# Retention and expert layer on one core: three chunks held for the products by token tiles, rows of the gathered tile spread anew

## The chip, the cores and the metric

The kernel runs on one core of one Trainium2 chip. The metric is the time of one execution on the device in microseconds (us); less is better. Three runs of the kernel before gave 1871.47, 1871.71 and 1877.47 us, a median of 1871.71 us.

## The reference

One layer of a token generator with 512 tokens of width 1024 and 256 context tokens. Two token mixers (retention and a gated linear recurrence) are merged and projected; the result `x1` goes through a normalisation and into an expert layer, and a last normalisation follows. Only the expert layer and the last normalisation matter here:

```python
q = (xb @ wq).reshape(PEER_BLOCK, PEER_HEADS, 2, PEER_DHALF)
s = jnp.einsum('thpd,hpkd->thpk', q, keys)
s1, i1 = lax.top_k(s[:, :, 0], K)
s2, i2 = lax.top_k(s[:, :, 1], K)
cand = (s1[..., :, None] + s2[..., None, :]).reshape(PEER_BLOCK, PEER_HEADS, K * K)
top, ci = lax.top_k(cand, K)
e = take(i1, ci // K) * PEER_NKEYS + take(i2, ci % K)
g = jax.nn.softmax(top, axis=-1)
act = jax.nn.gelu(jnp.einsum('thkd,td->thk', u_tab[e], xb))
return jnp.einsum('thk,thkd->td', g * act, v_tab[e])
...
x = x + g2x * peer_ffn(hx2, ...)
return rms_norm(x, final_g)
```

Every token picks 128 (8 heads, 16 each) of 16384 experts; `u_tab` and `v_tab` hold one row of 1024 float32 values for each expert. All arithmetic is float32.

## The kernel before, in words

The 512 tokens are four tiles of 128. **Three tiles** (384 tokens, `ndt` = 3) take the expert layer as dense products over all 16384 experts, in 128 chunks of 128 experts. **The fourth tile** gathers the rows that its tokens picked: 128 rows of `u` (one for each of the 128 picks, 128 tokens at a time), then 128 rows of `v`.

A dense float32 product is made of three products of split operands (`mm3`): `split` writes the high part on ScalarE (ACT) and the low part on VectorE (DVE), and TensorE (PE) multiplies high by high, high by low and low by high.

*The first table, S stages (`s_stage`).* Stage j loads 512 KB of `uT`, splits them (`wh`, `wl`; `w` has 2 buffers, `wh` and `wl` 4), makes 24 products into one of two PSUM buffers `pS`, and ACT writes their gelu into `gt`, a ring of `RING` buffers. Chunks below `SPILL` are stored from there to DRAM (`gd`) and come back later as `gr`; the others stay in the ring until their chunk is used. So stage j needs the ring buffer of stage j - RING, and the PSUM buffer of stage j - 2.

*The table stage (lines 846 to 906).* For each dense tile, in 8 slots of 16 tokens, DVE makes four one-hot tiles (`ohB`, `ohAl`, `ohAh`, `ohAl`), PE multiplies them (`pw`, 32 products of 128 columns in a slot), ACT copies the weights into `stg`, and SyncE's queue (SP) stores 1 MB of them in DRAM (`wd`). S stages are woven in as the tiles go. The order of the tiles is 0, 1, 3, 2: at the third place stand the lists of the gathered tile (`gather_prep`), and with the last dense tile the first `GFIRST` rows of `u` are gathered, by GpSimd's queue (POOL) into one of 4 buffers `row`, 512 KB each, and multiplied on DVE.

*The product stage (lines 952 on).* For each of 128 chunks: its weights `wt` or `wu` (a table of 8 chunks, 1.5 MB read from `wd`, which waits for every store into `wd`), its gelus, their product `af`, the split `ah`, `al`; 512 KB of `v`, split into `vwh`, `vwl`; 18 products of 512 columns into `po`, 6 for each tile. S stages still to be made and rows still to be gathered are woven in: `done < GFIRST + GSTEPS * (n_ + 1) // 128`, that is 1.97 rows a chunk. Chunks 126 and 127 are held: their products are made tile by tile, and behind a tile's last one follows its `finish`: times `g2r`, plus `x1`, square and sum, root, times the reciprocal and `fgr`, and out. The gathered tile's `finish` comes when its rows are through.

The order of the instructions on each engine is set when the program is built, by a scheduler that plays the program through with its own durations. On the chip each engine runs its list in that order.

Of the kernel before, what the change touches and what calls it, by code (L numbers as in the profile page):

```python
# [11 lines left out]
F32 = mybir.dt.float32  # L12
F32R = mybir.dt.float32r
# [3 lines left out]
AF = mybir.ActivationFunctionType  # L17
OP = mybir.AluOpType
# [3 lines left out]
D = 1024  # L22
KT = 8
# [15 lines left out]
    _n += _w  # L39
NCOLS = _n  # L40
DT = 384
SPILL, RING = 52, 14
GFIRST, GSTEPS, SSTEPS = 10, 252, 124
AHEAD = 2
NROW = 4
TORD = (0, 1, 3, 2)
# [6 lines left out]
def block_kernel(ctx: ExitStack, tc: tile.TileContext, A):  # L53
    nc = tc.nc
    V, S, PE, G, SY = nc.vector, nc.scalar, nc.tensor, nc.gpsimd, nc.sync

    def f(ap):
        return ap.bitcast(F32)

    def split(hi, lo, src):  # L60
        S.activation(hi, src, AF.Copy)  # L61
        V.tensor_tensor(lo, src, f(hi), op=OP.subtract)  # L62

    def mm3(out, wh, wl, xh, xl, start, stop):
        PE.matmul(out, wh, xh, start=start, stop=False)  # L65
        PE.matmul(out, wh, xl, start=False, stop=False)  # L66
        PE.matmul(out, wl, xh, start=False, stop=stop)  # L67
# [5 lines left out]
    wst = ctx.enter_context(tc.tile_pool(name="wst", bufs=2, reuse_waits="tile"))  # L73
    wsp = ctx.enter_context(tc.tile_pool(name="wsp", bufs=4, reuse_waits="tile"))
# [8 lines left out]
    def load_split(src, st, sp):  # L83
        n, m = src.shape[1:]
        w = st.tile([128, n, m], F32, name="w", tag="w")
        SY.dma_start(w, src)
        wh = sp.tile([128, n, m], F32R, name="wh", tag="wh")
        wl = sp.tile([128, n, m], F32R, name="wl", tag="wl")
        split(wh, wl, w)
        return wh, wl  # L90
# [52 lines left out]
    hl = hp.tile([128, KT, NX], F32R, name="hl", tag="hl")  # L143
# [393 lines left out]
    with ExitStack() as es:  # L537
# [25 lines left out]
        for c in range(KT):  # L563
            for g, (sh_, sl_) in ((1, (lruh, lrul)), (0, (reth, retl))):
                if (c, g) not in early:
                    gate_tanh(c, g, mg)
                t = gates[c, g]
# [24 lines left out]
        for q, (pool, th, tl) in enumerate(((lm, "lruh", "lrul"), (mg, "reth", "retl"))):  # L592
            wo.append([pool.tile([128, 4, KT, 128], F32R, name=f"wo{t}", tag=t, bufs=1) for t in (th, tl)])
            for c in range(4):
                w = wst.tile([128, KT, 128], F32, name="w", tag="w")
# [6 lines left out]
        for hf in range(2):  # L602
# [29 lines left out]
            for c in range(0, KT, 2):  # L632
                pt = ps_of("ptok", psW)
                for i in range(2):
                    for q in range(2):
                        o = 128 * (2 * q + i)
# [124 lines left out]
    def s_more(n=1):  # L761
        nonlocal s_next
        for _ in range(n):
            if s_next < 128:
                s_stage(s_next)
                s_next += 1
# [28 lines left out]
    def gather_rows():  # L795
        for j in range(128):
            row = gp.tile([128, D], F32, name="row", bufs=4)
            G.indirect_dma_start(out=row, out_offset=None, in_=A["u"],  # L798
                                 in_offset=bass.IndirectOffsetOnAxis(ap=ei[:, j:j + 1], axis=0))
            V.scalar_tensor_tensor(row, row, 1.0, h2t, op0=OP.mult, op1=OP.mult, accum_out=act[:, j:j + 1])  # L800
            yield
        S.activation(act, act, AF.Gelu_apprx_tanh)
        V.tensor_tensor(act, act, gg, op=OP.mult)
        for j in range(128):
            row = gp.tile([128, D], F32, name="row", bufs=4)
            G.indirect_dma_start(out=row, out_offset=None, in_=A["v"],  # L806
                                 in_offset=bass.IndirectOffsetOnAxis(ap=ei[:, j:j + 1], axis=0))
            if j == 0:
                V.tensor_scalar(acc, row, act[:, j:j + 1], None, op0=OP.mult)
            else:  # L810
                V.scalar_tensor_tensor(acc, row, act[:, j:j + 1], acc, op0=OP.mult, op1=OP.add)  # L811
            yield

    with ExitStack() as es:
# [5 lines left out]
        for h0 in range(0, H, HG):  # L820
# [3 lines left out]
            for hf in range(2):  # L824
# [4 lines left out]
                for i, pq in enumerate(pqs):  # L829
# [4 lines left out]
                    for tt in range(2):  # L834
                        t = 2 * hf + tt
# [16 lines left out]
        gen = None  # L852
        for t in TORD:
            if t == ndt:
                gather_prep(p1)
                gen = gather_rows()
# [15 lines left out]
            for tg in range(128 // WG):  # L872
                stg = p1.tile([128, 128, WG], F32, name="stg", bufs=2)
                for t0 in range(0, WG, 16):
                    o = tg * WG + t0
# [31 lines left out]
    ph = gpx.enter_context(tc.tile_pool(name="ph", bufs=1, reuse_waits="tile"))  # L907
# [4 lines left out]
    def finish(t, src, xt):  # L912
        xo = gp.tile([128, D], F32, name="xo", tag="row", bufs=4)
        ss = gp.tile([128, 2], F32, name="ss", bufs=4)
        hs = [slice(512 * n, 512 * n + 512) for n in range(2)]
        for n, o in enumerate(hs):
            V.tensor_tensor(xo[:, o], src[:, o], g2r[:, o], op=OP.mult)
            V.tensor_tensor(xo[:, o], xo[:, o], xt[:, o], op=OP.add)
            S.activation(xt[:, o], xo[:, o], AF.Square, accum_out=ss[:, n:n + 1])
        V.tensor_tensor(ss[:, 0:1], ss[:, 0:1], ss[:, 1:2], op=OP.add)  # L920
        S.activation(ss[:, 0:1], ss[:, 0:1], AF.Sqrt, scale=1.0 / D, bias=epsc)
        V.reciprocal(ss[:, 0:1], ss[:, 0:1])
        for o in hs:
            V.scalar_tensor_tensor(xo[:, o], xo[:, o], ss[:, 0:1], fgr[:, o], op0=OP.mult, op1=OP.mult)
            SY.dma_start(A["out"][0, 128 * t:128 * t + 128, o], xo[:, o])

    def load_x1(t):
        if t in (1, 2):
            xt = ph.tile([128, D], F32, name="xt", tag="vw", bufs=2)
        else:  # L930
            xt = gp.tile([128, D], F32, name="xt", tag="row", bufs=4)
        SY.dma_start(xt, x1d[:, t])
        return xt
# [5 lines left out]
    order, q = [], 0  # L939
# [6 lines left out]
    def table(j):  # L946
        gr = j // WI
        if gr not in wts:
            wt = ph.tile([128, NG_, WI, WG], F32, name="wt" if WI * gr + WI > SPILL else "wu", bufs=2)
            SY.dma_start(wt, wd[:, :, WI * gr:WI * gr + WI, :])  # L950
            wts[gr] = wt
        return wts[gr]
# [3 lines left out]
    for n_, j in enumerate(order):  # L956
        ring = j >= SPILL
        while s_next < min(128, s_first + (128 - s_first) * (n_ + 1) // SSTEPS) or (ring and s_next <= j):
            s_more()
        if ring:  # L960
            a = Gs.pop(j)
        else:
            a = ph.tile([128, DT], F32, name="gr", bufs=2)
            SY.dma_start(a, gd[:, j])
        wt = table(j)
        v = ph.tile([128, D], F32, name="vw", bufs=2)
        vd = SY.dma_start(v, A["v"][128 * j:128 * j + 128])

        with tc.issue_after(vd.ins):
            table(order[min(n_ + 3, 127)])  # L970
        vh, vl = (ph.tile([128, D], F32R, name=f"vw{m}", bufs=2) for m in "hl")
        ah, al = (ph.tile([128, DT], F32R, name=f"a{m}", bufs=2) for m in "hl")
        split(vh, vl, v)
        af = ph.tile([128, DT], F32, name="af")
        paced = V.tensor_tensor(af.rearrange("p (g t) -> p g t", t=WG), a.rearrange("p (g t) -> p g t", t=WG), wt[:, :, j % WI], op=OP.mult)
        split(ah, al, af)
        last.append((ah, al, vh, vl))
        if n_ == 125:

            g2r, fgr = (wst.tile([128, KT, 128], F32, name=nm, tag="w").rearrange("p n m -> p (n m)") for nm in ("g2r", "fgr"))  # L980
            SY.dma_start(g2r, g2d.to_broadcast([128, D]))
            SY.dma_start(fgr, A["fg"].to_broadcast([128, D]))
            with tc.issue_after(paced.ins):
                S.activation(gp.tile([128, 1], F32, name="ws"), epsc, AF.Sqrt)
        if n_ != 126:
            for t in range(ndt):
                for n in range(2):
                    for i, (ah, al, vh, vl) in enumerate(last):
                        mm3(outs[t][:, 512 * n:512 * n + 512], ah[:, 128 * t:128 * t + 128], al[:, 128 * t:128 * t + 128],
                            vh[:, 512 * n:512 * n + 512], vl[:, 512 * n:512 * n + 512], n_ == 0, n_ == 127 and i == 1)  # L990
                if n_ == 127:
                    finish(t, outs[t], load_x1(t))
            last = []
        with tc.issue_after(paced.ins):
            while gen and done < GFIRST + GSTEPS * (n_ + 1) // 128:
                done += 1
                if next(gen, 1):
                    gen = None
                    finish(ndt, acc, load_x1(ndt))
# [64 lines left out]
```

## Time and profile before

| | |
|---|---|
| median of the three runs | 1871.71 us |
| profiled execution, its own time | 1868.65 us |
| span of its instructions | 1866.9 us |
| PE busy | 1812.8 us (97%) |
| DVE busy | 1511.8 us (81%) |
| ACT busy | 822.2 us (44%) |
| moved by DMA | 431.27 MB, 231 GB/s on the mean |

The profile is that of one execution. "Busy" counts the time in which an instruction of the engine ran; products on PE overlap, so the step from one start to the next is shorter than an instruction's length: a product of 384 columns starts every 0.17 us and lasts 0.34 us. "Idle before" a row, in square brackets, is time in which its engine did nothing, with what ended it. L61 is line 61 of the kernel. SPq rows are DMAs issued by SP.

### The profile page before, as it was taken

Reading aid. Unit: us, or ns where it says so; the run is one execution under the profiler, and the core shown is the slowest. Engines: PE = TensorE matmul, PEld = TensorE weight load, DVE = VectorE, ACT = ScalarE, POOL = GpSimd, SP = SyncE. Lnnn points to the kernel's source line nnn. Section 1 sums busy time; section 2 is a strip of 40 time slices with the busy share of each in tenths; the row PEclk is TensorE's granted clock in tenths of the full one; section 3 lists DMA queues with packets and bytes.
Section 4 is the critical chain, followed back from the end, with each engine's and each line's share of the span. In section 5 each row is a group of like instructions: output and inputs, shape, how many; then the busy total and the mean of one; then the engine's idle time right before and its main releaser. Section 6 shows DMA issues by size and latency. Waiting matters only on the chain.

```text
span 1866.9 us, 26880 instructions
## 1 busy us (share of the span) xinstructions
PE 1812.8 (97%) x9953; PEld 1598.3 (86%) x9953; DVE 1511.8 (81%) x2793; ACT 822.2 (44%) x1203; POOL 377.7 (20%) x327
## 2 busy tenths in 40 slices
PE   7899999999999999999999989999999999999997
PEld 3788888887878989999999978888888888888886
DVE  8988777788853679999988678877787878788788
ACT  4666575765222444445545433333333333333323
POOL 0000000000000000000031244444454444344440
PEclk9999999999999999999999999999999999999999
DMA  7122121215953433657778989999999899998985
GB/s 312 52 68 69 57 69 57 69 57 175 327 157 102 153 107 105 189 188 246 253 283 281 320 323 348 337 330 320 345 339 344 316 340 339 355 329 320 347 308 206
DMA packets 173320, 431.27 MB, mean 231 GB/s; under 512 B 14850, under 2 KB 84610, under 8 KB 168708
## 3 DMA queue, kind: packets, MB, share of 16 engines
q1 hardware_dynamic: 136324, 295.31, 47.0%
q0 software_dynamic: 36864, 134.23, 19.7%
q8 instruction: 78, 1.28, 0.3%
q14 instruction: 54, 0.44, 0.1%
HBM read 388.86 MB, written 40.64 MB: 230 GB/s over the span
## 4 chain that ended last, share of the span: by engine, by line
PE 75%; DVE 11%; DMA 9%; ACT 2%; issue 2%; SPq 0%; DVEq 0%; POOL 0%; ACTq 0%; POOLq 0%
PE po L65 9%; PE po L66 9%; PE po L67 9%; PE pS L65 8%; PE pS L66 8%; PE pS L67 8%; DMA vw<-in_v_dram 5%; DMA modb<-in_mod_t_dram 2%; DVE wl L62 2%; PE pw L893 1%; PE pw L894 1%; PE pu L66 1%; PE pu L67 1%; PE pu L65 1%; PE p L66 1%
## 5 line engine op out<-in xcount | busy, mean ns | idle before, releaser
L61 ACT ACTIVATE wh<-w 128x1024 fp32r<-128x1024 f32 (+1 forms) x216 | 224.9, 1043 | 340.8 <-PE pS L66 76.9
L65 PE MATMUL pS<-h2h,wh 128*128 128x384 f32 x1024 | 346.5, 338 | 2.4 <-ACT gt L753 2.2
L67 PE MATMUL pS<-h2h,wl 128*128 128x384 f32 x1024 | 345.5, 337 | 0.7 <-DVE wl L62 0.7
L66 PE MATMUL pS<-h2l,wh 128*128 128x384 f32 x1024 | 345.5, 337 | 0.0
L62 DVE TENSOR_TENSOR wl<-w,wh 128x1024 fp32r<-128x1024 f32 (+1 forms) x216 | 258.9, 1200 | 84.3 <-ACT wh L61 81.9
L798 POOL DMA_INDIRECT row<-in_u_dram,ei x128 | 190.3, 1487 | 564.3 <-DVE row L800 288.3
L66 PE MATMUL po<-vwl,ah 128*128 128x512 f32 x768 | 300.2, 391 | 0.0
L67 PE MATMUL po<-vwh,al 128*128 128x512 f32 x768 | 299.8, 391 | 0.0
L65 PE MATMUL po<-vwh,ah 128*128 128x512 f32 x768 | 267.0, 395 | 10.1 <-ACT vwh L61 10.1
L61 ACT ACTIVATE ah<-af 128x384 fp32r<-128x384 f32 x128 | 67.1, 524 | 382.1 <-PE po L66 261.1
L806 POOL DMA_INDIRECT row<-in_v_dram,ei x128 | 177.6, 1387 | 224.4 <-DVE acc L811 193.1
L65 PEld LDWEIGHTS pS<-h2h,wh 128*128 128x128 f32 x1024 | 192.6, 188 | 9.6 <-ACT gt L753 3.3
L62 DVE TENSOR_TENSOR vwl<-vw,vwh 128x1024 fp32r<-128x1024 f32 x128 | 156.3, 1221 | 53.3 <-ACT vwh L61 53.1
L67 PEld LDWEIGHTS pS<-h2h,wl 128*128 128x128 f32 x1024 | 192.5, 188 | 6.2 <-DVE wl L62 1.0
L66 PEld LDWEIGHTS pS<-h2l,wh 128*128 128x128 f32 x1024 | 192.6, 188 | 5.4
L65 PEld LDWEIGHTS po<-vwh,ah 128*128 128x128 f32 x768 | 143.0, 188 | 37.0 <-ACT vwh L61 11.7
L61 ACT ACTIVATE vwh<-vw 128x1024 fp32r<-128x1024 f32 x128 | 134.6, 1051 | 84.7 <-DMA vw<-in_v_dram 79.3
L66 PEld LDWEIGHTS po<-vwl,ah 128*128 128x128 f32 x768 | 144.3, 188 | 27.6 <-DVE vwl L62 0.4
L67 PEld LDWEIGHTS po<-vwh,al 128*128 128x128 f32 x768 | 144.4, 188 | 27.3
L811 DVE SCALAR_TENSOR_TENSOR acc<-row,act,acc 128x1024 f32<-128x1024 f32 x127 | 162.5, 1280 | 4.4 <-DMA row<-in_v_dram,ei 4.2
L800 DVE SCALAR_TENSOR_TENSOR row<-row,h2t 128x1024 f32<-128x1024 f32 x128 | 153.4, 1219 | 1.7 <-DMA row<-in_u_dram,ei 1.5
L62 DVE TENSOR_TENSOR al<-af,ah 128x384 fp32r<-128x384 f32 x128 | 71.1, 556 | 79.2 <-ACT ah L61 78.9
(368 smaller groups left out, 3489.5 us busy)
## 6 DMA issues: line engine op xcount, KB each, us to landing
w<-in_uT_dram SPq DMA_DIRECT2D x128, 512.0 KB, 4.8
vw<-in_v_dram SPq DMA_DIRECT2D x128, 512.0 KB, 6.6
w<-in_w_in_dram SPq DMA_DIRECT2D x48, 512.0 KB, 3.6
wd<-stg SPq DMA_DIRECT2D x24, 1024.0 KB, 6.0
modb<-in_mod_t_dram SPq DMA_DIRECT2D x32, 512.0 KB, 5.2
wt<-wd SPq DMA_DIRECT2D x10, 1536.0 KB, 15.9
gd<-gt SPq DMA_DIRECT2D x52, 192.0 KB, 3.3
gr<-gd SPq DMA_DIRECT2D x52, 192.0 KB, 6.7
```

The costliest lines, as they stand in the source:

```text
L61: S.activation(hi, src, AF.Copy)
L62: V.tensor_tensor(lo, src, f(hi), op=OP.subtract)
L65: PE.matmul(out, wh, xh, start=start, stop=False)
L66: PE.matmul(out, wh, xl, start=False, stop=False)
L67: PE.matmul(out, wl, xh, start=False, stop=stop)
L798: G.indirect_dma_start(out=row, out_offset=None, in_=A["u"], in_offset=bass.IndirectOffsetOnAxis(ap=ei[:, j:j + 1], axis=0))
L800: V.scalar_tensor_tensor(row, row, 1.0, h2t, op0=OP.mult, op1=OP.mult, accum_out=act[:, j:j + 1])
L806: G.indirect_dma_start(out=row, out_offset=None, in_=A["v"], in_offset=bass.IndirectOffsetOnAxis(ap=ei[:, j:j + 1], axis=0))
L811: V.scalar_tensor_tensor(acc, row, act[:, j:j + 1], acc, op0=OP.mult, op1=OP.add)
L893: PE.matmul(pw[:, i], B[:, xg, :, xi], Ah[:, xg, :, xi], start=True, stop=False)
L894: PE.matmul(pw[:, i], B[:, xg, :, xi], Al[:, xg, :, xi], start=False, stop=True)
```

## The change

- `SPILL` 52 to 53 and `RING` 14 to 13: one chunk more goes through DRAM, one buffer less in the ring.
- `GFIRST` 10 to 26: 26 rows of `u` with the last dense tile. Then none for chunks 0 to 3, two a chunk to chunk 103, 36 over the 22 chunks after it (1.64 each), the last at chunk 125. `SSTEPS` 124 to 118: S stages are spread over fewer chunks.
- `HELD` = 3: chunks 125 to 127 are held for products by tiles. Their `v` comes through the buffers `w`, `wh`, `wl` that the S stages have left; `ah` and `al` get 3 buffers. `g2r` and `fgr` move into the buffers `vwh` and `vwl`.
- In `finish` the product with `fgr` comes ahead of the root, as a product of two tensors; the reciprocal of the root comes last, half of the columns on ACT (`Copy` with a scale), half on DVE.

```diff
-SPILL, RING = 52, 14
-GFIRST, GSTEPS, SSTEPS = 10, 252, 124
+SPILL, RING = 53, 13
+GFIRST, GSTEPS, SSTEPS = 26, 236, 118
+HELD = 3
...
+        for o in hs:
+            V.tensor_tensor(xo[:, o], xo[:, o], fgr[:, o], op=OP.mult)
...
+        S.activation(xo[:, hs[0]], xo[:, hs[0]], AF.Copy, scale=ss[:, 0:1])
+        V.tensor_scalar(xo[:, hs[1]], xo[:, hs[1]], ss[:, 0:1], None, op0=OP.mult)
         for o in hs:
-            V.scalar_tensor_tensor(xo[:, o], xo[:, o], ss[:, 0:1], fgr[:, o], op0=OP.mult, op1=OP.mult)
...
+        if n_ < 128 - HELD:
+            v = ph.tile([128, D], F32, name="vw", bufs=2)
...
+            vh, vl = (t.rearrange("p n m -> p (n m)") for t in
+                      load_split(A["v"][128 * j:128 * j + 128].rearrange("p (n m) -> p n m", m=128), wst, wsp))
...
-        if n_ == 125:
-            g2r, fgr = (wst.tile([128, KT, 128], F32, name=nm, tag="w")...
+        if n_ == 126:
+            g2r, fgr = (ph.tile([128, D], F32, name=nm, tag=tag, bufs=2) for nm, tag in (("g2r", "vwh"), ("fgr", "vwl")))
...
-        if n_ != 126:
+        if n_ < 128 - HELD or n_ == 127:
...
+        rows = min(2 * max(0, n_ - 3), 200 + max(0, n_ - 103) * (GSTEPS - 200) // 22)
         with tc.issue_after(paced.ins):
-            while gen and done < GFIRST + GSTEPS * (n_ + 1) // 128:
+            while gen and done < min(GFIRST + rows, 256 + n_ // 126):
```

The scheduler's order moves with it. Lines of the changed kernel stand one to nine further down (L62 and L63 for L61 and L62, L754 for L753, L801 for L800, L984 for L975).

**ACT, from the last slots of the table stage to the first split of the product stage.** `stg` are the weights of a slot (four copies), `gt` the gelu of an S stage, `wh` the split of the next `uT`, `ah` the first split of chunk 0. Before:

```order
L895 ACTIVATE stg<-pw 128x128x4 x3
L61 ACTIVATE wh<-w 128x1024
L895 ACTIVATE stg<-pw 128x128x4
L61 ACTIVATE wh<-w 128x1024
L753 ACTIVATE gt<-pS 128x384
L61 ACTIVATE wh<-w 128x1024
L753 ACTIVATE gt<-pS 128x384
L61 ACTIVATE wh<-w 128x1024
L753 ACTIVATE gt<-pS 128x384
L61 ACTIVATE ah<-af 128x384
L61 ACTIVATE vwh<-vw 128x1024
L753 ACTIVATE gt<-pS 128x384
```

After:

```order
L754 ACTIVATE gt<-pS 128x384 x2
L62 ACTIVATE wh<-w 128x1024 x2
L896 ACTIVATE stg<-pw 128x128x4 x8
L62 ACTIVATE wh<-w 128x1024 x3
L62 ACTIVATE ah<-af 128x384
L754 ACTIVATE gt<-pS 128x384
L62 ACTIVATE vwh<-vw 128x1024
```

Three gelus stood between the last `stg` and the first `ah`; now none does. On PE it is the same: before, 116 products of S stages 63 to 67 stand between the last product `pw` of the table stage and the first `po`; now stage 67 is through ahead of the last `pw`, and behind it stand 21 products of stage 68, which waits for the PSUM buffer of stage 66, that is for the gelu that ACT now has behind `ah`.

**DVE, over the same place.** `row,act` is one gathered row's product, `wl` a split of `uT`, `af` the first instruction of chunk 0. Before:

```order
L884 TENSOR_TENSOR ohB<-iota,e2T 128x2048
L885 TENSOR_TENSOR ohAl<-iota,e1T 128x2048
L800 SCALAR_TENSOR_TENSOR row,act<-row,h2t 128x1024 x2
L62 TENSOR_TENSOR wl<-w,wh 128x1024
L886 TENSOR_TENSOR ohAh<-ohAl,ghT 128x2048
L887 TENSOR_TENSOR ohAl<-ohAl,glT 128x2048
L62 TENSOR_TENSOR wl<-w,wh 128x1024 x5
L975 TENSOR_TENSOR af<-gt,wt 128x384
L800 SCALAR_TENSOR_TENSOR row,act<-row,h2t 128x1024
L62 TENSOR_TENSOR al<-af,ah 128x384
```

After:

```order
L885 TENSOR_TENSOR ohB<-iota,e2T 128x2048
L886 TENSOR_TENSOR ohAl<-iota,e1T 128x2048
L801 SCALAR_TENSOR_TENSOR row,act<-row,h2t 128x1024
L888 TENSOR_TENSOR ohAl<-ohAl,glT 128x2048
L801 SCALAR_TENSOR_TENSOR row,act<-row,h2t 128x1024 x2
L887 TENSOR_TENSOR ohAh<-ohAl,ghT 128x2048
L801 SCALAR_TENSOR_TENSOR row,act<-row,h2t 128x1024
L63 TENSOR_TENSOR wl<-w,wh 128x1024 x2
L888 TENSOR_TENSOR ohAl<-ohAl,glT 128x2048
L63 TENSOR_TENSOR wl<-w,wh 128x1024 x3
L984 TENSOR_TENSOR af<-gt,wt 128x384
L63 TENSOR_TENSOR al<-af,ah 128x384
```

Rows stand between the one-hot tiles of every slot now, and two of the five splits `wl` moved ahead of the last one-hot tile.

**DVE at the end.** Before, from the gathered tile's last step to the first tile's root:

```order
L924 SCALAR_TENSOR_TENSOR xo<-xo,ss,fgr 128x512 x2
L62 TENSOR_TENSOR al<-af,ah 128x384
L62 TENSOR_TENSOR vwl<-vw,vwh 128x1024
L917 TENSOR_TENSOR xo<-po_10702,g2r 128x512 x2
L918 TENSOR_TENSOR xo<-xo,xt 128x512 x2
L917 TENSOR_TENSOR xo<-po_10703,g2r 128x512 x2
L918 TENSOR_TENSOR xo<-xo,xt 128x512
```

After:

```order
L63 TENSOR_TENSOR al<-af,ah 128x384
L918 TENSOR_TENSOR xo<-acc,g2r 128x512 x2
L919 TENSOR_TENSOR xo<-xo,xt 128x512 x2
L922 TENSOR_TENSOR xo<-xo,fgr 128x512 x2
L923 TENSOR_TENSOR ss<-ss 128x1
L925 RECIPROCAL ss<-ss 128x1
L927 TENSOR_SCALAR xo<-xo,ss 128x512
L918 TENSOR_TENSOR xo<-po_10751,g2r 128x512 x2
L919 TENSOR_TENSOR xo<-xo,xt 128x512 x2
```

The gathered tile (`acc`) is finished behind the last chunk's splits and straight ahead of the first dense tile; before, it was finished among the last chunks. On PE, 16 products follow the first dense tile's last one before, 20 now; the third tile's are the last in both.

## Rows read from the trace of the kernel before

**Rows 1.** The page, head and part 1: span, PE's busy time.
```profile
span 1866.9 us, 26880 instructions
PE 1812.8 (97%) x9953; PEld 1598.3 (86%) x9953; DVE 1511.8 (81%) x2793; ACT 822.2 (44%) x1203; POOL 377.7 (20%) x327
```

**Rows 2.** Stretches: length, busy PE, PEld, DVE, ACT, POOL; PE clock, DMA share, GB/s.
```profile
940.00:1062.00 122.00, 122.00 (x960) 118.23 (x959) 93.38 (x111) 58.09 (x99) 21.94 (x15) 1.00 0.83 292
1062.00:1855.00 793.00, 782.92 (x3749) 685.02 (x3747) 643.83 (x818) 278.38 (x386) 337.72 (x242) 1.00 0.94 329
1855.10:1866.90 11.80, 0.04 (x1) 0.00 (x0) 8.29 (x19) 3.37 (x11) 0.00 (x0) 0.63 0.35 133
...
1480.00:1600.00 120.00, 117.81 (x563) 102.47 (x562) 98.35 (x106) 39.42 (x55) 53.45 (x39) 1.00 0.98 341
```

**Rows 3.** One stretch, instructions on `pS` alone: length, busy PE, PEld, DVE, ACT.
```profile
1042.30:1062.05 19.75, 19.75 (x114) 19.75 (x115) 0.00 (x0) 1.41 (x3) 1.00 0.93 304
```

**Rows 4.** Timeline between table stage and product stage: start, length, engine, line, what.
```profile
1042.26 0.22 PE L894 MATMUL pw<-ohAl,ohB 128*128 128x128 f16 x1
...
1044.95 0.58 ACT L895 ACTIVATE stg<-pw 128x512 f32<-128x512 f32 x1
...
1045.55 0.33 SPq L898 DMA_DIRECT2D wd<-stg  x1
...
1050.61 0.62 SPq L950 DMA_DIRECT2D wt<-wd  x1
...
1059.98 0.56 DVE L975 TENSOR_TENSOR af<-gt,wt 128x384 f32<-128x384 f32 x1 [3.30 <-DMA wt<-wd]
...
1060.57 0.53 ACT L61 ACTIVATE ah<-af 128x384 fp32r<-128x384 f32 x1 [4.77 <-DVE af L975]
...
1062.48 0.68 PE L65 MATMUL po<-vwh,ah 128*128 128x512 f32 x2
```

**Rows 5.** DMA issues: engine, count, KB each, median us to landing.
```profile
row<-in_u_dram,ei POOLq DMA_INDIRECT x128, 8.0
...
g2r<-g2d SPq DMA_DIRECT2D x1, 512.0 KB, 12.8
fgr<-in_fg_dram SPq DMA_DIRECT2D x1, 512.0 KB, 5.2
```

**Rows 6.** The tile `wt`: its ten loads, issue to landing.
```profile
DMA to landing us min/median/max: 9.3/15.9/20.1
```

**Rows 7.** Waits of PE from 1060 us on: us in total, times, longest.
```profile
PE po L65 <- ACT vwh L61: 10.1, 5, 5.9
```

**Rows 8.** Timeline ahead of the longest of these waits.
```profile
1065.44 0.61 SPq L950 DMA_DIRECT2D wt<-wd  x1
...
1067.34 8.36 SPq L967 DMA_DIRECT2D vw<-in_v_dram  x1
...
1086.17 1.06 ACT L61 ACTIVATE vwh<-vw 128x1024 fp32r<-128x1024 f32 x1 [9.44 <-DMA vw<-in_v_dram]
```

**Rows 9.** Two stretches behind that wait, columns as in Rows 2.
```profile
1087.20:1090.40 3.20, 3.12 (x9) 2.70 (x10) 2.64 (x3) 1.49 (x3) 0.00 (x0) 0.55 0.30 72
1090.40:1093.00 2.60, 2.60 (x13) 2.17 (x12) 2.56 (x5) 1.07 (x1) 0.31 (x1) 1.00 0.84 279
```

**Rows 10.** Groups by line: busy us, mean ns; `L573` with min/median/max ns.
```profile
L800 DVE SCALAR_TENSOR_TENSOR row<-row,h2t 128x1024 f32<-128x1024 f32 x128 | 153.4, 1219 | 1.7 <-DMA row<-in_u_dram,ei 1.5
...
L573 DVE TENSOR_SCALAR t<-t x8: 419/420/423, 465.4 to 605.7; 128x512 f32<-128x512 f32 x8
```

**Rows 11.** Timeline of the end: DVE's first and last work on `po`, PE's last product.
```profile
1851.54 1.29 DVE L917 TENSOR_TENSOR xo<-po,g2r 128x512 f32<-128x512 f32 x2 [2.21 <-PE po L67]
1852.74 1.28 DVE L918 TENSOR_TENSOR xo<-xo,xt 128x512 f32<-128x512 f32 x2
...
1854.75 0.39 PE L67 MATMUL po<-vwh,al 128*128 128x512 f32 x1
...
1862.05 1.41 DVE L924 SCALAR_TENSOR_TENSOR xo<-xo,ss,fgr 128x512 f32<-128x512 f32 x2
```

More of the change, by code (lines that the diff above doesn't have):

```diff
@@ L965, in block_kernel @@
         wt = table(j)
[L966 to L973, printed above, removed]
+        ah, al = (ph.tile([128, DT], F32R, name=f"a{m}", bufs=HELD) for m in "hl")
+        if n_ < 128 - HELD:
+            v = ph.tile([128, D], F32, name="vw", bufs=2)
+            vd = SY.dma_start(v, A["v"][128 * j:128 * j + 128])
+            with tc.issue_after(vd.ins):
+                table(order[min(n_ + 3, 127)])
+            vh, vl = (ph.tile([128, D], F32R, name=f"vw{m}", bufs=2) for m in "hl")
+            split(vh, vl, v)
+        else:
+            vh, vl = (t.rearrange("p n m -> p (n m)") for t in
+                      load_split(A["v"][128 * j:128 * j + 128].rearrange("p (n m) -> p n m", m=128), wst, wsp))
         af = ph.tile([128, DT], F32, name="af")
@@ L977, in block_kernel @@
         last.append((ah, al, vh, vl))
-        if n_ == 125:
-            g2r, fgr = (wst.tile([128, KT, 128], F32, name=nm, tag="w").rearrange("p n m -> p (n m)") for nm in ("g2r", "fgr"))
+        if n_ == 126:
+            g2r, fgr = (ph.tile([128, D], F32, name=nm, tag=tag, bufs=2) for nm, tag in (("g2r", "vwh"), ("fgr", "vwl")))
             SY.dma_start(g2r, g2d.to_broadcast([128, D]))
             SY.dma_start(fgr, A["fg"].to_broadcast([128, D]))
+        if n_ == 127 - HELD:
             with tc.issue_after(paced.ins):
                 S.activation(gp.tile([128, 1], F32, name="ws"), epsc, AF.Sqrt)
-        if n_ != 126:
+        if n_ < 128 - HELD or n_ == 127:
             for t in range(ndt):
@@ L989, in block_kernel @@
                         mm3(outs[t][:, 512 * n:512 * n + 512], ah[:, 128 * t:128 * t + 128], al[:, 128 * t:128 * t + 128],
-                            vh[:, 512 * n:512 * n + 512], vl[:, 512 * n:512 * n + 512], n_ == 0, n_ == 127 and i == 1)
+                            vh[:, 512 * n:512 * n + 512], vl[:, 512 * n:512 * n + 512], n_ == 0, n_ == 127 and i == HELD - 1)
                 if n_ == 127:
```

## The prediction

> **What bounds the kernel now.** I read the page's head first: PE is busy 97% of 1866.9 us [rows 1], so the question is where PE waits. The stretches [rows 2] show it. In the last part of the table stage, 940 to 1062, PE never stops (122 of 122 us), DVE is busy 93.4 us, and the DMA engines move 292 GB/s at a share of 0.83. In the product stage, 1062 to 1855, PE lacks 10.1 of 793 us, at 329 GB/s and a DMA share of 0.94. PE's waits name the cause of all 10.1 us: five times a `po` product stood for the split of a `v` chunk, once for 5.9 us [rows 7]; ACT had stood 9.4 us for that chunk's DMA, which SP had issued behind a table load [rows 8]. Behind that stop the granted clock was 0.55 for 3.2 us, most of it at the lower level of 1.2 GHz: 9 products started, which take 9 x 0.20 us at the pace of the 13 behind them, so another 1.4 us [rows 9]. After PE's last product, at 1854.75 + 0.39 = 1855.14, 11.8 us follow for the last normalisation [rows 2, 11]. What a change can win is thus about 11.5 us of stops and a part of 11.8 us. What it can lose is any cover that lies over a wait today, and one big cover does.
>
> **The cover.** The product stage needs a table that is read from DRAM behind the last store of the table stage. The timeline [rows 4] gives that chain: last `pw` product 1042.26; its weights copied by 1045.53; store issued 1045.55; landed, and the table's load issued, 1050.61; landed, and `af` of chunk 0, 1059.98; `ah` 1060.57; first `po` 1062.48. That is 20 us, and PE doesn't feel them: 114 recorded S products (116 by the order) fill 19.75 us of it without a gap [rows 3].
>
> **Rows and S stages in the table stage.** 16 more rows of `u` lie there. DVE takes 1.22 us for one [rows 10]: 19.5 us on top of 93.4 of 122, so DVE still fits, with 9 us over. But the one-hot tiles come later, and the order of PE answers with more S products ahead of the last `pw`: 68.0 stages instead of 63.1, 4.9 stages x 24 products x 0.173 us (19.75 / 114 [rows 3]) = 20.4 us. PE does the same work ahead of the first `po`; the last `pw` just moves to its end, to about 1062.7.
>
> **The boundary: the term that decides.** Behind the last `pw` PE's list now has stage 68, and that stage waits for a PSUM buffer that is free only when a gelu of stage 66 has run, whose `gt` buffer is free only when `af` of chunk 0 has run. ACT has that gelu behind `ah`. So PE stands from the last `pw` to that gelu's end; behind the waiting product all of PE's list is queued. The wait: the last copy 1.2 us after the last `pw` (four copies stand together now; before, the last stood behind a split that waited for its DMA, and took 3.3), store to landing 5.06, table load to `af` 9.37, `af` to `ah` 0.59, `ah` and gelu together 1.0: **17.2 us**. Bounds: the 9.37 is the shortest of ten such loads, whose median is 15.9 [rows 6], so 16 from below and 23.8 from above. I take the short one: it is the load of this same place, and SP holds the loads listed behind it back until the store has landed, now as before. After such a stop the clock restarts low, as in [rows 9]: +1.4. Together +18.6.
>
> The Trainium skill (DMA: Bandwidth & Descriptors, Anatomy of one DMA) prices a transfer at 2.0 us plus bytes over 436 GB/s, 5.6 us for this table of 1.5 MB, and the term would be 3.8 us less; this case's trace disagrees, with no load of the ten under 9.3 us [rows 6].
>
> **DMA in the table stage.** 16 rows x 0.524 MB = 8.4 MB more on 35.6 MB (122 us x 292) make 44.0 MB. No stretch of 120 us here moves more than 341 GB/s [rows 2]; at that rate they need 129 us, 7 us more than PE's work. A part can run on behind the last `pw`, while PE stands anyway, so I take +3, with 0 and +8 as ends (the upper end for rows that land late and hold up DVE's one-hot tiles, whose list they stand in; a row's landing takes 8.0 us [rows 5]).
>
> The Trainium skill (DMA: Bandwidth & Descriptors, Specifications) gives a core some 358 GB/s of HBM; by that this term would be 1 us. No 120 us here come near it; whether they could, no run shows.
>
> **The product stage.** 8.4 MB leave it, and chunks 0 to 3 have no rows. The stop at 1087, 5.9 + 1.4 us, came behind a second table, among gathered rows. The rows are gone; but the second table is now issued ahead of the second `v` chunk, and PE's order has only 4 S products between chunks 0 and 1. From the first table's landing, 2.1 MB (table and `v`) at 329 GB/s are 6.4 us at least, and 11 at the pace of the first table; PE has 21 x 0.173 + 18 x 0.23 = 7.7 us of work till then. I take a stop of 3 us in place of 7.3: -4.3 (ends -7.3 and 0). The four other stops, 4.2 us [rows 7], were of the same kind; in the middle there are 2 rows a chunk instead of 1.97, and S stages come faster, so transfers per PE time are the same; the end, with 1.64 rows, is easier. I take -1.4 (ends -4.2 and +4). The spilled chunk adds 0.4 MB, 1.2 us of DMA beside PE: nothing.
>
> **The end.** The first tile's last product stands 20 products ahead of PE's end instead of 16, not the 36 that "by tiles" suggests; 4 x 0.23 = 0.9 us earlier. DVE, which sets the end, works without a break from 1851.54 to 1863.46 [rows 11]. A tile's work on it was four tensor products at 0.60 (two start in 1.20) and two of 0.70; now six at 0.60 and one scale of 0.42 [rows 10], +0.2 a tile. The last step after the root falls from 1.41 to 0.42 beside ACT's half. I take -0.5. The gathered tile's `finish` now stands on DVE ahead of the first dense tile's, and `g2r` for it can be loaded only when chunk 123's products are done, 72 products, 72 x 0.23 = 16.5 us, ahead of PE's end. With the 5.2 us of `fgr` [rows 5] it lands 11 us ahead, its DVE work (3.6 + 0.4, root and table load about 2) is through 5 us ahead, just in time. With the 12.8 of `g2r` it costs 7 us. Ends -1.5 and +7.
>
> **The sum.** +18.6 + 3 - 4.3 - 1.4 - 0.5 = +15.4. On the profiled execution, 1868.65, that is 1884; the median lies 3.1 us above it, so 1887. I put 1886, since the low ends of two terms are the nearer ones.
>
> **Rivals.** *Not slower: the boundary at its lowest, and every stop gone.* The product stage keeps its rows short, all 11.5 us of stops vanish, the boundary costs 16 without a slow restart, the table stage nothing, the end -1.5: +3, 1875. For it speaks that all five stops name a `v` transfer and 8.4 MB leave; against it that the middle is as dense as before. It decides for "no change" below +5.6 us. To be faster, the boundary would have to be under 8 us, less than table load and copies alone; only a wait that I misread would do it (that stage 68 doesn't wait for the gelu). 13% for no change, 9% for faster.
>
> *Transfers take over in the table stage.* Rows and `uT` share a full DMA: the stage ends 8 us later, and the table load takes the median 15.9: 8 + 25.2 - 4.3 - 1.4 - 0.5 = +27, 1899. For it: 361 GB/s would be needed, over what any 120 us here show. Against: the rows can wait, and PE's S products have 4 split buffers. 15%.
>
> *The end waits for `g2r`*: +7 on the forecast, 1893. For it the 12.8 us, against it that this load met rows and `v` transfers, which are over by then. 8%.
>
> **How the numbers follow.** Forecast with its own range of 1877 to 1895: 55%. About 0.3%, 5.6 us, is what a measurement of this kernel can tell from no change. Slower 0.55 + 0.15 + 0.08 = 0.78, same 0.13, faster 0.09. The range leaves out the faster case, the low edge of the one without change and the upper half of the second rival, just under 2 in 10: 1869 to 1900.
>
> **What would show it.** In the profile after: PE idle once for 14 to 20 us at about 1063 to 1083, ahead of a `pS` product, ended by ACT's `gt`, with the wait of `af` for `wt` behind it; no S product between the last `pw` and that gap. GB/s in the 120 us ahead of it up from 292 to about 340. The stop behind the first chunk shorter than 7 us. DVE's first work on `po` 4.5 us ahead of PE's end, the end 11 to 11.5 us after it. The prediction is wrong if PE goes from `pw` to `po` without that gap, or if the last `pw` comes well ahead of 1060.

## The result, and the profile after

The changed kernel takes **1905.5 us**, the median of four runs (1901.1 to 1909.8); the kernel before took 1872.5 beside it. The ratio is 1.0166, with a 95% interval of 1.0145 to 1.0188; it is not the quotient of the two medians (1.0176), and in the table of the experiments the two can differ by 0.2%. The forecast was 1886, with a range of 1869 to 1900: the sign was right, and the time lies above the range.

Head and part 1 of its page, to be held against [rows 1]; PE is busy 10 us longer for the same number of products:

```profile
span 1908.0 us, 26901 instructions
PE 1822.8 (96%) x9953; PEld 1603.8 (84%) x9953; DVE 1513.8 (79%) x2797; ACT 825.2 (43%) x1207; POOL 377.7 (20%) x327
```

Stretches, columns as in [rows 2]: the 120 us up to the last `pw`, and the part of them that ran at half clock; the gap behind it; the product stage from the gap on, and its stretch behind one stop; the end.

```profile
950.00:1070.00 120.00, 114.52 (x841) 109.31 (x840) 97.43 (x125) 47.73 (x81) 41.52 (x26) 0.96 0.84 297
1062.00:1068.60 6.60, 6.24 (x21) 6.08 (x21) 1.02 (x1) 0.57 (x2) 0.00 (x0) 0.50 0.92 322
1070.90:1088.80 17.90, 0.16 (x3) 0.00 (x1) 4.55 (x5) 4.99 (x9) 0.00 (x0) 0.63 0.88 269
...
1088.80:1894.50 805.70, 789.53 (x3744) 688.31 (x3744) 625.42 (x787) 276.69 (x384) 320.99 (x226) 0.99 0.89 312
1188.80:1194.60 5.80, 5.80 (x15) 4.74 (x16) 5.77 (x10) 0.32 (x1) 2.91 (x2) 0.50 0.74 212
...
1894.60:1908.00 13.40, 0.00 (x0) 0.00 (x0) 8.99 (x22) 5.67 (x14) 0.00 (x0) 0.63 0.31 117
```

PE's waits from 1000 us on (us in all, times, longest), against [rows 7]:

```profile
PE pS L66 <- ACT gt L754: 18.4, 2, 17.7
PE po L66 <- ACT vwh L62: 14.2, 6, 3.6
PE pw L894 <- ACT stg L896: 2.8, 4, 2.1
PE pS L66 <- ACT wh L62: 2.1, 1, 2.1
PE po L67 <- DVE vwl L63: 1.9, 4, 0.8
```

The timeline of the boundary, against [rows 4]:

```profile
1070.84 0.22 PE L895 MATMUL pw<-ohAl,ohB 128*128 128x128 f16 x1
1072.02 0.33 SPq L899 DMA_DIRECT2D wd<-stg  x1
...
1076.06 0.62 SPq L954 DMA_DIRECT2D wt<-wd  x1
...
1087.25 0.56 DVE L984 TENSOR_TENSOR af<-gt,wt 128x384 f32<-128x384 f32 x1 [6.87 <-DMA wt<-wd]
1087.85 0.52 ACT L62 ACTIVATE ah<-af 128x384 fp32r<-128x384 f32 x1 [8.72 <-DVE af L984]
1088.27 0.47 ACT L754 ACTIVATE gt<-pS 128x384 f32<-128x384 f32 x1
...
1088.80 0.69 PE L66 MATMUL pS<-h2h,wh 128*128 128x384 f32 x1 [17.74 <-ACT gt L754]
```

**Where 41.1 us went** (1908.0 against 1866.9; medians differ by 33, since this profiled execution is the slowest of its runs). At 1062.48 [rows 4] PE had done before what it now has done at 1088.80: +26.3, of which 17.7 are the gap and 8.6 a late end of the table stage. (The two executions were not level when the table stage began: its first `pw` starts at 824.5 in the trace before and at 822.6 here. Counted from there the stage ends 10.5 us late. In the row of 120 us above, PE stands 5.5 us and the clock is 0.96 on the mean.) From there to PE's end it takes 1894.5 - 1088.8 = 805.7 us against 1855.1 - 1062.5 = 792.6: +13.1. Of these 6.0 are stops (14.2 + 1.9 against 10.1). About 6.6 are half clock: 3.6 us behind the gap, 5.8 behind the stop at 1188.8 (row above) and 6.9 behind one at 1283.4 ran at 0.50 to 0.51 (1.2 GHz), and about half of these 16.3 us is lost, 8 against 1.4 before. The end takes 13.5 us against 11.8: +1.7. Each trace is one execution, and executions of the kernel before alone lie between 1861 and 1878 us in the runs below. So a difference of a few microseconds between two traces is not firm; the ratios are.

### The profile page after: what moved, and what is told of

Read it like the earlier page. It is cut to its first block, busy times and chain, and to the rows that moved or that the text cites. A ratio compares the mean times of both kernels' runs of the same rounds, so it can differ in the third digit from the quotient of the medians.

```text
span 1908.0 us, 26901 instructions
## 1 busy us (share of the span) xinstructions
PE 1822.8 (96%) x9953; PEld 1603.8 (84%) x9953; DVE 1513.8 (79%) x2797; ACT 825.2 (43%) x1207; POOL 377.7 (20%) x327
## 5 line engine op out<-in xcount | busy, mean ns | idle before, releaser
L62 ACT ACTIVATE wh<-w 128x1024 fp32r<-128x1024 f32 (+1 forms) x219 | 227.8, 1043 | 362.3 <-PE pS L67 84.8
L63 DVE TENSOR_TENSOR wl<-w,wh 128x1024 fp32r<-128x1024 f32 (+1 forms) x219 | 263.3, 1204 | 80.5 <-ACT wh L62 76.6
L67 PE MATMUL po<-vwl,ah 128*128 128x512 f32 x750 | 295.6, 394 | 1.9 <-DVE vwl L63 1.9
L68 PE MATMUL po<-vwh,al 128*128 128x512 f32 x750 | 294.6, 393 | 0.0
L66 PE MATMUL po<-vwh,ah 128*128 128x512 f32 x750 | 270.3, 396 | 14.3 <-ACT vwh L62 14.2
L62 ACT ACTIVATE ah<-af 128x384 fp32r<-128x384 f32 x128 | 67.0, 524 | 353.8 <-PE po L67 340.6
L63 DVE TENSOR_TENSOR vwl<-vw,vwh 128x1024 fp32r<-128x1024 f32 x125 | 152.6, 1221 | 38.7 <-ACT vwh L62 38.5
L62 ACT ACTIVATE vwh<-vw 128x1024 fp32r<-128x1024 f32 x125 | 131.4, 1052 | 111.0 <-DMA vw<-in_v_dram 106.5
L801 DVE SCALAR_TENSOR_TENSOR row<-row,h2t 128x1024 f32<-128x1024 f32 x128 | 152.0, 1220 | 7.8 <-DMA row<-in_u_dram,ei 7.8
L63 DVE TENSOR_TENSOR al<-af,ah 128x384 fp32r<-128x384 f32 x128 | 71.1, 555 | 90.5 <-ACT ah L62 86.9
```

## The experiments

All ratios are to the kernel before, run on the same chip. Of each run one execution is traced. No run has `HELD` = 3 by itself.

| run | what it is | us | ratio (95%) |
|---|---|---|---|
| e9_after_again | the whole change | 1902.1 | 1.0174 (1.0143 to 1.0205) |
| e1_rows_back | all of it but the rows | 1882.3 | 1.0052 (1.0027 to 1.0077) |
| e2_rows_only | the rows alone | 1898.0 | 1.0138 (1.0095 to 1.0181) |
| e5_ssteps | SSTEPS alone | 1868.1 | 0.9990 (0.9970 to 1.0009) |
| e6_spill | SPILL and RING alone | 1885.4 | 1.0083 (1.0064 to 1.0102) |
| e3_s_held | the change, S products held back | 1901.1 | 1.0174 (1.0135 to 1.0212) |
| e4_rows_behind | the change, 16 rows behind the table stage | 1881.3 | 1.0063 (1.0040 to 1.0086) |
| e7_no_loads | the change, 16 rows not loaded | 1902.7 | 1.0178 (1.0161 to 1.0195) |
| e8_parts | before, tables in four parts | 1854.8 | 0.9925 (0.9908 to 0.9942) |
| e12_parts_scale | e8 and the new finish | 1857.5 | 0.9934 (0.9912 to 0.9956) |
| e11_back_parts | e1, tables in four parts | 1859.2 | 0.9944 (0.9925 to 0.9964) |
| e10_after_parts | the change, tables in four parts | 1879.7 | 1.0049 (1.0030 to 1.0068) |

### Which part costs: the rows put back, and the rows alone

e1 undoes the row schedule in the changed kernel; e2 makes it in the kernel before.

```diff
-GFIRST, GSTEPS, SSTEPS = 26, 236, 118
+GFIRST, GSTEPS, SSTEPS = 10, 252, 118
...
-            while gen and done < min(GFIRST + rows, 256 + n_ // 126):
+            while gen and done < min(GFIRST + GSTEPS * (n_ + 1) // 128, 256 + n_ // 126):
```

> The changed kernel with the rows spread as in the kernel before (10 rows of u with the last dense tile, then 252/128 a chunk); HELD = 3, the scale behind the root, SPILL 53, RING 13 and SSTEPS 118 stay. In the order 115 S products stand between the last pw and the first po again. Theory A (the rows ahead of the table's chain are what costs): the gap of 17.7 us, the restart at half clock behind it (1.8) and the late end of the table stage (8.5) go, 28 us in all; of the 10.9 us by which the rest of the product stage is longer, the part that belongs to the rows goes too: 1872 to 1878. Theory B (the product stage is longer because S stages, tables and the held chunks stand otherwise, whatever the rows do): those 10.9 us and the 1.7 at the end stay: 1885.

> The kernel before with nothing but the new spread of the rows (26 with the last dense tile, none for chunks 0 to 3, then two a chunk, 36 over the 22 chunks behind chunk 103). Theory A: PE stands once for 16 to 20 us behind the last pw, ahead of an S product that waits for a gelu, and the last pw comes 6 to 9 us late: 1872 + 17.7 + 1.8 + 8.5 = 1900, and the 5 us up to the changed kernel's 1905.5 are the other parts'. Theory B (the loss is shared: the boundary is the rows', the table stage's and product stage's the other parts'): 1872 + 19.5 = 1892.

PE's waits, e1 first, then e2:

```profile
PE po L66 <- ACT vwh L62: 14.0, 6, 4.3
PE po L67 <- DVE vwl L63: 2.7, 2, 2.4
```

```profile
PE pS L65 <- ACT gt L753: 16.7, 1, 16.7
PE po L65 <- ACT vwh L61: 13.5, 9, 3.5
PE pw L893 <- ACT stg L895: 2.9, 4, 2.3
PE pS L65 <- ACT wh L61: 1.5, 1, 1.5
```

With the rows put back the gap is gone and the last `pw` starts at 1042.3, as before. The rows alone bring the gap and the late stage, and e2's 1898.0 us lies near the 1900 of theory A. So theory A holds for those. Yet e1 is no 1872 to 1878: some 10 us remain (0.52%), with 16.7 us of stops instead of 10.1 and an end of 13.6 us. That is theory B's share, and no step of the prediction had it.

### What delays the table's chain

e3 makes two S stages fewer in the slots (63 instead of 65) and holds the products of stages 63 and 64 until the last `pw` (`held[0]`); the later stages follow behind them:

```diff
+            if held:
+                es.enter_context(tc.issue_after(held[0]))
             for k in range(KT):
                 mm3(ps[:, :DT], uh[:, k], ul[:, k], ...)
```

> The changed kernel with the products of S stages 63 and later kept behind the last pw: 102 S products, 17.6 us of PE, stand there again, the rows stay where the change put them. Theory A1 (the S products that were used up ahead of the last pw are the loss): the gap of 17.7 us and its restart go and nothing takes their place: 1886. Theory A2 (DVE's list sets the last one-hot tile, at 1063 in the changed kernel against 1038.6 before, so PE has nothing else to do and the gap only moves ahead of the last pw): PE stands 10 to 15 us in all in front of pw products between 1000 and 1064, the last pw comes at 1064 to 1066, the first po 17.9 us behind it at 1082 to 1084 against 1092: 1895 to 1898.

e4 issues 16 rows behind the last one-hot tile (`lo`); e7 leaves 16 transfers out, and with them 16 activations of the gathered tile:

```diff
-                        while done < GFIRST * gslot // (8 * (ndt - TORD.index(ndt))):
+                        while done < 10 * gslot // (8 * (ndt - TORD.index(ndt))):
...
+        with tc.issue_after(lo.ins):
+            while done < GFIRST:
+                done += 1
+                next(gen)
```

> The changed kernel with 10 rows ahead of the last one-hot tile as before the change and the other 16 issued behind it, while the table's chain runs; in the order 137 S products (23.8 us of PE) stand between the last pw and the first po. Theory A2 (only what stands ahead of the last one-hot tile on DVE delays the chain): last one-hot at about 1039, no gap of more than 3 us at the boundary, and the product stage has 16 rows fewer than before: 1870 to 1877. Rival C (transfers: 16 rows are 8.4 MB, 25 us at 341 GB/s, beside the table of 1.5 MB and the uT loads): the table takes 16 to 20 us in place of 9.4 to 11.2, the chain 24 to 28 us against 23.8 of cover, a stop of up to 4 us and late uT: 1877 to 1884.

```diff
+            src = row
+            if 10 <= j < 26:
+                src = h2t
+            else:
+                G.indirect_dma_start(out=row, ...)
...
-            V.scalar_tensor_tensor(row, row, 1.0, h2t, ...)
+            V.scalar_tensor_tensor(row, src, 1.0, h2t, ...)
```

> The changed kernel without the gather of rows 10 to 25 of u: DVE multiplies h2t by itself in their place, so those 16 activations of the gathered tile are not the reference's; DVE's list and the S products ahead of the last pw stay. 8.4 MB of transfers leave the table stage. Theory F (transfers made the end of the table stage late): DVE's waits for rows and PE's stops of 2.3 and 2.6 us at 1058 and 1061 with the half clock behind them go, the last pw comes 8 us sooner, at 1062 to 1063, and the last one-hot tile at 1058 to 1060; the gap of 17 us at the boundary stays: 8 us less than the changed kernel, a ratio of 1.012 to the kernel before. Theory G (DVE's own time for 16 rows, 19.5 us, does it): the last one-hot tile stays at 1061 to 1063 and the last pw above 1066: 1.016.

PE's waits in e3:

```profile
PE po L66 <- ACT vwh L62: 10.8, 7, 3.3
PE pw L899 <- DVE ohAh L892: 7.8, 1, 7.8
PE pw L900 <- DVE ohAl L893: 5.3, 2, 5.1
PE pS L66 <- ACT gt L759: 2.1, 1, 2.1
```

The gap behind the last `pw` is gone and 13.1 us of waiting for one-hot tiles stand ahead of it: theory A2, though the last `pw` (1059.0) and the first `po` (1079.3) come 3 to 7 us sooner than it said and the time, 1901.1, is 3 us above its range. The S products were not taken from the cover at a loss; PE had nothing else to do while DVE, with 16 rows more on its list, came to the last one-hot tile. The starts of that tile, in the kernel before, the changed kernel and e7:

```profile
1037.35 1.23 DVE L887 TENSOR_TENSOR ohAl<-ohAl,glT 128x2048 f16<-128x2048 f16 x1
```

```profile
1061.80 1.22 DVE L888 TENSOR_TENSOR ohAl<-ohAl,glT 128x2048 f16<-128x2048 f16 x1
```

```profile
1052.59 1.22 DVE L892 TENSOR_TENSOR ohAl<-ohAl,glT 128x2048 f16<-128x2048 f16 x1
```

These traces, too, were not level when the table stage began: the first `pw` starts at 824.5, 822.6 and 820.2 us in the three (820.1 in e9, 822.5 in e3). Counted from there, the last one-hot tile comes 26.4 us later in the changed kernel, and 19.5 us later when the 16 rows are computed but not loaded. That is about DVE's own time for them, as theory G has it: 16 x 1.22 = 19.5 us [rows 10], or 18 by the step of 1.14 from one row to the next. The rest, 6.8 us here and 5.1 in e9, where the tile starts at 1057.5, goes when the loads go. It is not the rows' loads alone, though: e3 has them and holds S products back, and there the tile is 19.9 us late.

In the changed kernel DVE once waited 2.41 us for a row, and PE stood 2.06 us for `wh` and 2.11 for `stg`, after which S products ahead of the last `pw` ran at half clock (1062.00:1068.60 above). Without the 16 loads PE hardly stands in the 120 us up to the last `pw`, and the clock stays up; e7, columns as in [rows 2]:

```profile
940.00:1060.00 120.00, 119.09 (x921) 114.57 (x919) 104.41 (x135) 52.94 (x87) 16.82 (x10) 1.00 0.70 246
```

So transfers made the end of the table stage late, as theory F has it. But its 8 us did not come: e7 has no better time than e9. Its gap grows to 21.6 us, since the store goes out 3.0 us behind the last `pw` (1.2 in the changed kernel), with a split of `uT` that waited for its load ahead of the copies on ACT, and takes 7.6 us to land. Its profiled execution is 15 us below that of e9, its median equal; what the transfers are worth in time stays open.

e4 has the last `pw` at 1042.24 and 140 S products behind it. SP's rows there:

```profile
1045.47 0.42 SPq L899 DMA_DIRECT2D wd<-stg  x1
...
1057.14 0.62 SPq L958 DMA_DIRECT2D wt<-wd  x1
```

The store took 11.7 us to land among the rows, against 5.1 [rows 4], the table 12.9, and PE stood 8.4 us: more than rival C's 4 us, while the time of 1881.3 lies in C's range. The chain can be stretched from both sides, by work ahead of it on DVE and by transfers beside it.

### What lengthens the product stage

```diff
-GFIRST, GSTEPS, SSTEPS = 10, 252, 124
+GFIRST, GSTEPS, SSTEPS = 10, 252, 118
```

> The kernel before with SSTEPS 118 in place of 124 and nothing else. The run with the rows put back was 9.8 us over the kernel before, about 1.8 of it at the end, 8 in stops of the product stage. Theory D (the S stages that are made sooner put more uT loads among the v transfers, and that is where the 8 us are): 1876 to 1880 where the kernel before takes 1869 to 1872, that is +6 to +9. Theory E (the stops come from where the tables of both kinds fall, which SPILL sets): within 3 us of the kernel before.

```diff
-SPILL, RING = 52, 14
+SPILL, RING = 53, 13
```

> The kernel before with SPILL 53 and RING 13 and nothing else; the table borders of 8 chunks fall elsewhere in the order of the chunks, and one chunk more goes through DRAM. Theory E (where two tables are loaded within some 12 us of each other, a v transfer stands behind them): stops move and add up to 14 to 17 us against 10.1, +6 to +9 over the kernel before. Theory D (SSTEPS is the cause): within 3 us of the kernel before.

SSTEPS costs nothing that is seen. SPILL and RING alone cost **16 us**, the largest thing the prediction missed: theory E, but with 20.7 us of stops where it said 14 to 17. It is no fixed price: e1 has the same SPILL and RING and lies 0.52% over the kernel before, e6 0.83%, with intervals that just overlap. e6's waits, and its longest stop:

```profile
PE po L65 <- ACT vwh L61: 16.4, 9, 4.4
PE po L66 <- DVE vwl L62: 4.3, 4, 2.4
```

```profile
1263.66 0.54 SPq L950 DMA_DIRECT2D wu<-wd  x1
1264.89 7.92 SPq L967 DMA_DIRECT2D vw<-in_v_dram  x1
...
1283.20 1.06 ACT L61 ACTIVATE vwh<-vw 128x1024 fp32r<-128x1024 f32 x1 [11.46 <-DMA vw<-in_v_dram]
1284.31 1.65 PE L65 MATMUL po<-vwh,ah 128*128 128x512 f32 x3 [4.45 <-ACT vwh L61]
```

A `v` chunk issued 1.2 us behind a table comes 18 us later; the median in this run is 6.4. The table itself landed 18.1 us after its issue, at 1281.8, just ahead of the chunk. SP stood 7.9 us in the chunk's issue, which mostly takes 0.33, so the loads listed behind it went out late too. In the changed kernel the stop at 1188.8 has the same form, behind two tables issued at 1154.8 and 1167.2. With SPILL 53 the first ring chunks cross a border of 8 sooner and the other borders shift, so tables stand ahead of other `v` chunks; that this is how SPILL makes the stops is argued here, and tested below by cutting the tables. That two tables must fall together, as the expectation put it, is not borne out: this stop stands behind one.

The Trainium skill (DMA: Bandwidth & Descriptors, Two DMAs through the same engine are not ordered) says that descriptors of one queue start in order on an engine. The rows above agree: the chunk's 512 KB wait for the 1.5 MB ahead of them on SP's queue, while rows on POOL's queue kept landing in 6.0 to 10.6 us.

So the table was cut. e8, e10 and e11 load it in four parts, each behind another chunk's `v`:

```diff
-                table(order[min(n_ + 3, 127)])
+                for p in range(NP):
+                    part(order[min(n_ + 3 + NP - 1 - p, 127)], p)
...
+            o = slice(NG_ // NP * p, NG_ // NP * (p + 1))
+            SY.dma_start(wts[gr][:, o], wd[:, o, WI * gr:WI * gr + WI, :])
```

> The kernel before with each table of 8 chunks loaded in four parts of 0.4 MB, issued 6, 5, 4 and 3 chunks ahead behind the v transfers of four chunks, in place of one load of 1.5 MB 3 chunks ahead. Theory H (a v transfer is late where it stands behind a whole table of 1.5 MB on the queue): the stops of 10.1 us fall to 2 to 5, with the half clock behind the first: 6 to 9 us less than the kernel before, 0.996. Rival I (the DMA engines are full over the whole stage, share 0.94 to 0.98, and the order of the transfers doesn't matter): within 3 us of the kernel before, stops of 8 to 12 us at other places.

> The changed kernel with the tables loaded in four parts, 6 to 3 chunks ahead, and nothing else. Theory H (a v transfer behind a whole table makes the stops of the product stage): stops of 14 to 17 us fall to under 4, with the half clock behind them (6 us) too; the gap at the boundary stays at 15 to 20 us, perhaps 2 to 4 shorter since the first table's four parts are loaded beside each other (9.8 us from issue to af where the parts were tried, 9.4 before, 11.2 after the change); the end stays at 13.1 to 13.6: 18 to 23 us less than the changed kernel, 1.005 to 1.009. Rival I (the transfers of the changed product stage don't fit in any order): stops of 8 us or more stay, 1.011 or more.

> The changed kernel with the rows spread as before the change and the tables in four parts: SPILL 53, RING 13, SSTEPS 118, three held chunks and the new end stay. Theory K (what SPILL 53 costs it costs only through whole tables that fall badly): the stops are under 4 us as in the kernel before with its tables in parts (0.9925), and only the end, 13.1 to 13.6 us against 11.8, is left of the change: 0.9925 + 0.001 = 0.993 to 0.995. Rival L (the ring of 13 buffers or the chunk more through DRAM costs by itself): stops of 8 us or more, 0.999 or more.

PE's waits in e8, e10 and e11, in full, and e8's product stage in one stretch:

```profile
PE po L66 <- DVE vwl L62: 1.3, 2, 0.9
```

```profile
PE pS L66 <- ACT gt L754: 18.5, 2, 18.3
PE pw L894 <- ACT stg L896: 4.7, 5, 2.5
```

```profile
PE po L66 <- ACT vwh L62: 2.5, 1, 2.5
PE po L67 <- DVE vwl L63: 2.1, 1, 2.1
```

```profile
1059.20:1840.60 781.40, 780.11 (x3747) 683.54 (x3745) 644.39 (x816) 275.90 (x384) 337.14 (x241) 1.00 0.94 334
```

Theory H holds: the stops fall from 10.1 to 1.3 us at the same DMA share of 0.94, and from 16.1 to none with the change. The time of e8 falls by 14.7 us, more than the 6 to 9 expected. Of the 14.5 us between the traces 11.2 lie in the product stage; 3.3 lie ahead of the first `pw`, where no table has been loaded yet. e8 does two things at once, it makes the loads smaller and issues most of them earlier, and no run has one without the other. Theory K holds within the intervals: e11 is 0.2% over e8, with the intervals overlapping, and 1.1 us of it is the end (12.9 us against 11.8), so with tables in parts nothing more is seen of SPILL 53, RING 13 and the held chunks. What the rows cost is left: 1.0049 - 0.9944 = 1.05%, 20 us, with the gap of 18.3 us untouched. **e8 is faster than both kernels**, by 0.75% than the one before.

### The end

e12 makes only the new order in `finish`, on top of e8.

```diff
+        for o in hs:
+            V.tensor_tensor(xo[:, o], xo[:, o], fgr[:, o], op=OP.mult)
...
+        S.activation(xo[:, hs[0]], xo[:, hs[0]], AF.Copy, scale=ss[:, 0:1])
+        V.tensor_scalar(xo[:, hs[1]], xo[:, hs[1]], ss[:, 0:1], None, op0=OP.mult)
-            V.scalar_tensor_tensor(xo[:, o], xo[:, o], ss[:, 0:1], fgr[:, o], op0=OP.mult, op1=OP.mult)
```

> The kernel before with the tables in four parts and of the change only the new order in finish: fgr ahead of the root, then the scale, half on ACT and half on DVE; two chunks held, g2r and fgr where they were. Theory M (the end is longer because three chunks are held and g2r comes late): PE's end to the last instruction takes 11.3 to 11.9 us, as the kernel before has it: 0.9920 to 0.9930. Theory N (the product with fgr, now six instructions more on DVE, which sets the end, is the cause): 12.5 to 13.3 us, 0.993 to 0.994; it is read from the trace, since the times can't tell 1 us.

The stretch behind PE's last product, e8 and e12 (columns as in [rows 2]), and the last DVE instruction of e12:

```profile
1840.70:1852.40 11.70, 0.00 (x0) 0.00 (x0) 8.19 (x19) 3.38 (x11) 0.00 (x0) 0.63 0.35 134
```

```profile
1840.15:1854.55 14.40, 0.00 (x0) 0.00 (x0) 9.49 (x22) 5.33 (x15) 0.00 (x0) 0.64 0.29 109
```

```profile
1849.22 0.48 DVE L926 TENSOR_SCALAR xo<-xo,ss 128x512 f32<-128x512 f32 x1
```

The new `finish` alone makes the end 2.7 us longer, theory N and more: DVE works 1.3 us longer (9.49 against 8.19), and its list puts products of the later tiles ahead of the first tile's scale (that tile's root is done at 1844.0, its scale starts at 1847.4). So the three scales on DVE start within 2 us of each other, and four output transfers are issued one behind the other from 1849.1 to 1850.5. The ratios of e8 and e12 can't tell this; the ends of the five traced kernels with the old `finish` are 11.7 to 12.2 us. The end of the runs with the new one and three held chunks is 12.9 to 13.6 us, so three held chunks are not seen to lengthen it.

### The whole change once more

> The changed kernel once more, unchanged, beside the next three on one chip. Theory J (the parts add: rows 1.0138, SPILL 53 with RING 13 1.0083, SSTEPS 0.999, the end 1.8 us): a ratio of 1.017 to 1.022; in the trace a gap of 16 to 22 us at the boundary and stops of 12 to 17 us in the product stage. A rival that the row spread and SPILL overlap (fewer rows among the first two tables) puts it at 1.013 to 1.016.

The ratio of 1.0174 lies in theory J's range, with a gap of 18.2 us as it said; the 19.5 us of stops are above its 12 to 17. The parts, 1.38 + 0.83 - 0.10 = 2.1% without the end, come to a little more than the 1.7% of the whole. Whether they overlap the intervals don't tell.

## Why the prediction was wrong, step by step

The sum was +15.4; the two traces differ by 41.1: boundary 19.5 against 18.6, table stage 8.6 against 3, product stage 11.3 against -5.7, end 1.7 against -0.5. The step that failed is the product stage.

- **The boundary** (+18.6): right. PE stood 17.7 us (18.2 and 18.3 in e9 and e10) against 17.2, ended by the gelu that was named, with `af`, `ah` and `gt` in that order behind the table's landing; 3.6 us at half clock behind it, 1.8 lost against 1.4. Two misses partly cancel in it: the table's load took 11.2 us to `af` instead of 9.4, and store to landing 4.0 instead of 5.1. (The 5.6 us that the prediction cites from the Trainium skill is a fit for transfers that GpSimd issues; SP issues this one.)
- **"The last `pw` just moves to its end", DVE "still fits", DMA +3:** too small, 8.6 where the bound was +8; counted from the first `pw`, 10.5 and in e9 8.2. DVE did fit into the time, and its list put the last one-hot tile 24.6 to 26.4 us later, of which a fifth to a quarter went with the loads (e7). The transfers showed in PE's waits and the half clock ahead of the last `pw`, not in the rate: GB/s did not rise to 340 over 120 us (297).
- **The product stage (-5.7):** the step that failed; +13.1 less the 1.8 of restart that the boundary has. The stop at 1087, 7.3 us with its half clock, went whole, where the prediction kept 3 us. (At the pace it names, 1.57 MB in 9.37 us, 2.1 MB take 12.5 us and not 11, so it should have kept 4.8.) The failed term is the -1.4 for the four other stops, with +4 as its upper end: their 4.2 us became 16.1, at 1188, 1283, 1316 and 1547 above all, and two of them were followed by 12.7 us at half clock, some 6.4 us lost: +18 in all. Two readings stood behind that term. "The spilled chunk adds 0.4 MB: nothing" priced the bytes of SPILL and RING, not where they put the tables in SP's queue: e6, +16 us. And fewer rows were to make it easier: e2 has 13.5 us of stops for `vwh`, all behind 1100, where the kernel before has 4.2. At 0.94 of the DMA engines the stops were a matter of which transfer stands in front of which, as e8 and e10 show. The half clock was counted behind one stop; it came behind the gap and two more.
- **The end (-0.5):** wrong in sign, +1.7. The 0.2 a tile was the right size for each instruction; that DVE's list interleaves the tiles so that the scales come late and together was not seen. The gathered tile did wait 2.6 us for `g2r` ahead of it.
- **The rivals:** transfers taking over gave 1899, nearest in time, and for a part of its reason: the table stage ended 8.6 us late, but the first table did not take 15.9 us, and the 13 us of the product stage stood in no rival.

## What to carry to other kernels

Work that is moved ahead of the first link of a DRAM round trip can cost its whole time there if the engine that feeds that link has a list in order: here 16 rows of 1.22 us on DVE put the link 19.5 us later, and e3 shows that it made no difference on which side of the link PE kept its other work. On a queue with little slack a parameter that moves the borders of large loads is a change of its own: list which small load then stands behind which large one, or cut the large load and issue its parts behind several small ones. Put a price on where a transfer stands, not on its bytes alone.

## What the runs showed of the hardware

At the same DMA share (0.94) and nearly the same rate (334 against 329 GB/s), the same bytes in smaller loads and another order took 781.4 us instead of 792.6, with 1.3 us of stops instead of 10.1. An issue on SP directly behind a table stood 7.9 us (e6, at 1264.89) and 12.1 us (the changed kernel, at 1167.80), where one of these issues takes 0.33 us in the median. The granted clock stood at 0.50, the lower level, for 5.8 us behind a stop of 3.6 us, but not behind every stop of that length: the one at 1316.0, also 3.6 us, was followed by the full clock.
